# A depthwise convolution of 31 taps moved from the vector engine to the tensor engine, and a recurrence's inputs made ahead, in a two-layer hybrid backbone

## The chip, the cores and the metric

The kernel runs on one core of one Trainium2 chip. The metric is the device time of one execution in microseconds (us), as the median of several runs. The engines are TensorE (PE, with its weight loads as PEld), VectorE (DVE), ScalarE (ACT), GpSimd (POOL) and SyncE (SP), whose queue issues nearly all DMAs.

## The reference, cut to what matters

Each of two layers joins four groups of heads behind one input projection. Layer 0 has 1024 latent and 256 context tokens; layer 1 puts out the latent ones alone. The parts that the change touches are the recurrence (a), the convolution module (c), and around them the attention (b) and the Hyena inputs (d):

```python
p = h @ w_in[l]
y_a = rglru_mixer(p[..., :OFF_B], ...)       # short convolution, gates, scan in both directions
y_b = diff_attn_mixer(p[..., OFF_B:OFF_C], ...)
y_c = conformer_conv(p[..., OFF_C:OFF_D], *conf)
y_d = hyena_mixer(p[..., OFF_D:], ...)
...
def conformer_conv(pc, conv_w, conv_b, ln_g, ln_b, w_pw, b_pw):
    u = pc[..., :W_C] * jax.nn.sigmoid(pc[..., W_C:])        # W_C = 256 channels
    u = dwconv(u, conv_w, conv_b, (CONF_K // 2, CONF_K // 2))   # CONF_K = 31 taps, one filter a channel
    u = layer_norm(u, ln_g, ln_b)
    return jax.nn.silu(u) @ w_pw + b_pw
```

The context is convolved by itself, so zeros stand between it and the latent tokens. Behind these follow the output projection and a mixture of experts.

## The kernel before

Channels lie on the 128 partitions and tokens along the free axis. `phase1` (L2028) does the input projection, the recurrence and the attention of a layer. `win` (L1044) projects one block of 128 output channels: it loads 512 KB of weights (`wir`), splits them on ACT into a rounded high part `wih` and on POOL into the rest `wil`, and for each group of 512, 512 and 256 tokens issues 24 matmuls (8 slices of the inner dimension, three products of high and low parts) into one accumulator `mm`; a function given with it then evacuates the accumulator. In the projections there are five accumulators `mm`, and three named `rg` for the recurrence and what follows.

The order in the program is: block 0; the recurrence for channels 0 to 127 (`recur(0)`); blocks 12 and 10, then 13 and 11, whose evacuation `glu_evac` writes the gated linear unit into an SBUF tile `cu`; block 2 with `gate(0, h)`; block 1 and the recurrence for channels 128 to 255; queries, keys and values; `gate(1, h)`; and last `conv31` for both channel blocks.

`rglru` (L1377) goes through three pieces for each of two directions. In each it makes `rg_u` by a convolution of 4 taps (one instruction on POOL, three on DVE), multiplies it on PE with two gate matrices (L1407), and goes on over ACT, POOL and a scan on DVE. The tile `rg_u` has one buffer. `conv31` (L1444) runs 31 instructions on DVE over all tokens (1295 columns in layer 0, 1024 in layer 1), each adding one tap to `cacc`, and stores the result in `cd`, which `conformer` (L1464) reads later for the layer norm.

The attention (L1153) follows with its own accumulators and a single `mm`, which the Hyena rows 14 to 19 (`rest`, L2091) and in layer 0 a part of the next layer's modulation (`modulation`, L954, L979) use in turn. Behind it `hyena_in` (L1713) loads `hx`, convolves it on POOL and DVE into `hu` and transposes it on PE into an `rg` accumulator, and `conformer` and the Hyena transforms (`tabc`, `H`) follow.

The order of the instructions on each engine is made by a scheduler when the kernel is built: of the instructions that are ready by its own reckoning it takes the one that stands first in the program. So an instruction that stands late can run early where its engine has room. On the chip each engine then works strictly in its order.

## Time and profile before

| what | value |
|---|---|
| median of 3 runs | 3575.4 us (3574.82 to 3578.94) |
| profiled execution, time | 3583.19 us |
| profiled execution, span of its instructions | 3581.3 us |
| PE busy | 3073.7 us, 86% |
| DVE busy | 2274.8 us, 64% |
| ACT busy | 1564.7 us, 44% |
| POOL busy | 722.5 us, 20% |
| mean granted PE clock | 0.923 |

Busy time is the union of an engine's instructions. Ends of matmuls are modelled, so a busy PE isn't PE at its peak; the distance from one matmul's start to the next tells its pace. The granted clock is the share of PE's full clock in a stretch; its two levels are 1.2 and 2.4 GHz, 0.5 and 1.0. All times below are counted from the start of the span.

### The profile page before, as it was taken

What the parts mean: (1) busy time and instruction counts of PE and PEld (TensorE: products, weight loads), DVE (VectorE), ACT (ScalarE), POOL (GpSimd) and SP (SyncE); (2) the same over time, 40 slices, a digit from 0 to 9 for tenths busy, and PEclk for the clock granted to TensorE, in tenths of its full rate; (3) what the DMA queues carried; (4) which work ended last, traced back from release to release, by engine and by line L of the source; (5) the groups of instructions that cost most, each with busy time, mean ns of one, the idle gap of its engine ahead of it and who ended that gap; (6) DMA issues with size and microseconds to landing.
All of it is one profiled execution on the core that took longest, in us unless ns stands there. A gap on an engine that the chain in (4) does not pass through costs nothing. (4 is left out here: it accounts for less than half of the span.)

```text
span 3581.3 us, 43827 instructions
## 1 busy us (share of the span) xinstructions
PE 3073.7 (86%) x14952; PEld 2071.0 (58%) x14952; DVE 2274.8 (64%) x3297; ACT 1564.7 (44%) x2537; POOL 722.5 (20%) x579
## 2 busy tenths in 40 slices
PE   5798888997899699999997587799779799899993
PEld 1246665775678354676554465667657655465551
DVE  6674885787768433476543778588876653355626
ACT  4234334772334233455543444377323343344533
POOL 2212451003210111111110435300330111111102
PEclk8899899998999699999999798899899899999996
DMA  5752226215565888987878512311546489988796
GB/s 185 230 192 61 69 90 212 70 39 191 161 210 174 286 305 307 369 292 258 318 254 322 170 40 92 135 57 46 174 145 230 151 287 379 378 283 285 270 349 236
DMA packets 415375, 743.33 MB, mean 208 GB/s; under 512 B 46219, under 2 KB 181240, under 8 KB 415146
## 3 DMA queue, kind: packets, MB, share of 16 engines
q1 hardware_dynamic: 397546, 702.69, 56.6%
q0 software_dynamic: 17600, 37.79, 3.1%
q8 instruction: 119, 1.95, 0.2%
q14 instruction: 110, 0.90, 0.1%
HBM read 656.13 MB, written 105.30 MB: 213 GB/s over the span
## 5 line engine op out<-in xcount | busy, mean ns | idle before, releaser
L679 DVE TENSOR_TENSOR wl<-wr,wh 128x1024 fp32r<-128x1024 f32 (+1 forms) x440 | 516.2, 1203 | 395.8 <-ACT wh L678 382.8
L678 ACT ACTIVATE wh<-wr 128x1024 fp32r<-128x1024 f32 (+1 forms) x440 | 442.1, 1038 | 331.5 <-PE mm L730 192.6
L734 PE MATMUL mm<-wr,xl 128*64 128x512 f32 x1216 | 327.6, 607 | 3.4 <-DVE xl L690 1.6
L1065 PE MATMUL mm<-hh,wih 128*128 128x512 f32 (+1 forms) x752 | 290.6, 387 | 13.8 <-ACT stg L1129 8.3
L1065 PE MATMUL mm<-hh,wil 128*128 128x512 f32 (+1 forms) x752 | 289.4, 386 | 10.5 <-POOL wil L951 9.7
L730 PE MATMUL mm<-wh,xh 128*128 128x512 f32 x704 | 288.7, 411 | 6.8 <-ACT wh L678 6.2
L1065 PE MATMUL mm<-hl,wih 128*128 128x512 f32 (+1 forms) x752 | 289.9, 386 | 1.5 <-DVE hl L951 1.0
L730 PE MATMUL mm<-wl,xh 128*128 128x512 f32 x704 | 278.4, 395 | 3.9 <-DVE wl L679 3.8
L730 PE MATMUL mm<-wh,xl 128*128 128x512 f32 x704 | 277.4, 394 | 0.0
L790 POOL DMA_INDIRECT fd<-ot,ridx x82 | 94.3, 1150 | 843.0 <-ACT ot L786 261.0
L1451 DVE SCALAR_TENSOR_TENSOR cacc<-cu,cw,cacc 128x1295 f32<-128x1295 f32 (+1 forms) x120 | 194.5, 1621 | 1.9
L671 POOL DMA_INDIRECT gb<-h2d,ridx x82 | 98.3, 1199 | 466.9 <-PE tr L698 177.9
L730 PEld LDWEIGHTS mm<-wh,xh 128*128 128x128 f32 x704 | 133.0, 189 | 92.6 <-issue 45.1
L1199 DVE TENSOR_REDUCE m<-A 128x1 f32<-128x1024 f32 x128 | 156.2, 1220 | 44.6 <-PE A L1189 36.6
L951 POOL TENSOR_TENSOR wil<-wir,wih 128x1024 fp32r<-128x1024 f32 x34 | 92.5, 2722 | 431.0 <-ACT wih L948 375.3
L734 PEld LDWEIGHTS mm<-wr,xl 128*64 128x64 f32 x1216 | 95.2, 137 | 141.8 <-issue 124.4
L1065 PEld LDWEIGHTS mm<-hh,wih 128*128 128x128 f32 x752 | 147.0, 196 | 44.9 <-ACT stg L1129 11.9
L1065 PEld LDWEIGHTS mm<-hh,wil 128*128 128x128 f32 x752 | 147.5, 196 | 39.1 <-POOL wil L951 10.9
L1065 PEld LDWEIGHTS mm<-hl,wih 128*128 128x128 f32 x752 | 147.4, 196 | 30.8 <-issue 6.2
L780 PE MATMUL mm<-wr,hl 128*64 128x512 f32 x608 | 154.9, 604 | 0.0
L1244 ACT ACTIVATE wT<-TR 128x512 f32<-128x512 f32 (+1 forms) x200 | 104.9, 524 | 108.2 <-PE TR L1239 99.1
L730 PEld LDWEIGHTS mm<-wl,xh 128*128 128x128 f32 x704 | 133.6, 190 | 30.5 <-DVE wl L679 6.7
(491 smaller groups left out, 6527.4 us busy)
## 6 DMA issues: line engine op xcount, KB each, us to landing
wr<-in_moe_w_gate_dram SPq DMA_DIRECT2D x256, 512.0 KB
wr<-in_moe_w_up_dram SPq DMA_DIRECT2D x256, 512.0 KB
wr<-in_moe_w_down_dram SPq DMA_DIRECT2D x256, 512.0 KB
wada<-in_w_ada_dram SPq DMA_DIRECT2D x48, 512.0 KB
tabc<-in_k_t_c_dram SPq DMA_DIRECT2D x88, 256.0 KB
wir<-in_w_in_dram SPq DMA_DIRECT2D x40, 512.0 KB
wr<-in_w_ada_dram SPq DMA_DIRECT2D x32, 512.0 KB
ks<-qkd SPq DMA_DIRECT2D x16, 640.0 KB
```

What stands on the lines that cost most here:

```text
L671: self.K.nc.gpsimd.indirect_dma_start(out=g[s, :D // (1 + h)], out_offset=None, in_=self.h2d[h], in_offset=bass.IndirectOffsetOnAxis(ap=id ...
L678: nc.scalar.activation(hi, src, AF.Copy)
L679: nc.vector.tensor_tensor(lo, src, hi.bitcast(FT), op=OP.subtract)
L730: nc.tensor.matmul(ps[b][w], x(k), y[:, kk], start=(k == 0 and c == 0), stop=(k == 7 and c == 2))
L734: nc.tensor.matmul(ps[b][0][w * 64:(w + 1) * 64], self.XT[n0 + b](k), raw[w][:, kk], start=(k == 0), stop=(k == 7))
L780: nc.tensor.matmul(po[b][0][o * 64:(o + 1) * 64], HT[b][:, k], raw[:, o], start=(k == 0), stop=(k == 3))
L790: s = nc.gpsimd.indirect_dma_start(out=self.fd[h], out_offset=bass.IndirectOffsetOnAxis(ap=ridx[r], axis=0), in_=ot[r], in_offset=None, bo ...
L951: (eng or nc.vector).tensor_tensor(lo, src, hi.bitcast(FT), op=OP.subtract)
L1065: nc.tensor.matmul(p[:, :n], a[:, k], b[:, k, t0:t0 + n], start=(k == 0 and a is wh and b is hh), stop=(k == 7 and a is wl))
L1199: nc.vector.tensor_reduce(m[:, c, 1:2], A[c], axis=AX.X, op=OP.max, negate=True)
L1244: nc.scalar.activation(o, i_, AF.Copy)
L1451: nc.vector.scalar_tensor_tensor(a, u[:, j:j + N], cw(j), a, op0=OP.mult, op1=OP.add)
```

## The change

The 31 taps are applied on PE. The gated linear unit no longer stays in SBUF: `glu_evac` stores each group in a DRAM buffer `ud` with zeros before, between and behind the two token ranges. `conv31` goes in pieces of 256 tokens. It loads a piece four times, shifted by 0 to 3 tokens, so that the 128 rows of a matmul are 32 channels at four shifts; 8 such matmuls, 4 tokens apart, add up the taps for 32 channels, and four groups of 32 channels write to the four quarters of the accumulator's partitions. The weights (`taps`) are made on the chip: a transpose, and a product with a pattern of ones on POOL. Ten pieces in layer 0 and eight in layer 1, with two buffers `cu`, now stand behind the Hyena rows in the attention's part of the program. A DVE instruction adds the bias and evacuates.

The recurrence's 4-tap convolution is a function of its own, `rglru_conv`, with six buffers `rg_u`, and comes before the GLU blocks' projection; block 1 comes before the second GLU pair, and `gate(0)` moves behind the first queries, keys and values. `stg` has three buffers in place of two.

```diff
@@ setup
-        self.cd = self.dram.tile([2 * P, T0 + 15], FT, name="cd")
+        self.cd = self.dram.tile([2 * P, T0], FT, name="cd")
+        self.ud = self.dram.tile([2 * P, UW], FT, name="ud")
...
+        for o, n in ((0, 15), (15 + TL, 15), (30 + T0, 16)):
+            nc.sync.dma_start(self.ud[:, o:o + n].rearrange("(b p) t -> p b t", p=P), z[:, :, :n])
@@ glu_evac
-            nc.vector.scalar_tensor_tensor(u[:, o:o + n], th[0][:, :n], 1.0, p[:, :n], op0=OP.add, op1=OP.mult)
+            t = th[0][:, :n]
+            nc.vector.scalar_tensor_tensor(t, t, 1.0, p[:, :n], op0=OP.add, op1=OP.mult)
+            nc.sync.dma_start(self.ud[b * P:(b + 1) * P, o:o + n], t)
@@ rglru
+    PIECES = [[(TL, TL + 3, TC), (0, 0, 512), (512, 512, 512)], [(TL, TL + 3, TC), (512, 512, 512), (0, 0, 512)]]
+
+    def rglru_conv(self, l, w, b, xa):
+        nc, res = self.nc, []
+        for s in range(3):
+            for d in range(2):
+                t0, a, n = self.PIECES[d][s]
...
+                u = w.tile([P, 512], FT, name="rg_u", bufs=6)[:, :n]
+                nc.gpsimd.tensor_scalar(u, xa[:, o:o + n], cw(0), self.pc("a_conv_b", d * 2 + b), op0=OP.mult,
+                                        op1=OP.add)
+                for j in range(1, 4):
+                    nc.vector.scalar_tensor_tensor(u, xa[:, o + j:o + j + n], cw(j), u, op0=OP.mult, op1=OP.add)
+                res.append(u)
+        return res
...
-        h = [w.tile([P, T0], FT, name=f"h{d}") for d in range(2)]
+        h = [w.tile([P, T0], FT, name=f"h{d}", bufs=2 - d) for d in range(2)]
...
-                u, r, i, t = (w.tile([P, 512], FT, name="rg_" + x, bufs=1 + (x != "u"))[:, :n] for x in "urit")
-                nc.gpsimd.tensor_scalar(u, xa[:, o:o + n], cw(0), self.pc("a_conv_b", c), op0=OP.mult, op1=OP.add)
-                for j in range(1, 4):
-                    nc.vector.scalar_tensor_tensor(u, xa[:, o + j:o + j + n], cw(j), u, op0=OP.mult, op1=OP.add)
+                u = us[s * 2 + d]
+                r, i, t = (w.tile([P, 512], FT, name="rg_" + x, bufs=2)[:, :n] for x in "rit")
@@ conv31
-        a = w.tile([P, N], FT, name="cacc")
...
-        nc.vector.tensor_scalar(a, u[:, 0:N], cw(0), self.pc("c_conv_b", b), op0=OP.mult, op1=OP.add)
-        for j in range(1, 31):
-            nc.vector.scalar_tensor_tensor(a, u[:, j:j + N], cw(j), a, op0=OP.mult, op1=OP.add)
-        nc.sync.dma_start(self.cd[b * P:(b + 1) * P, :N], a)
+    def taps(self, l, b, w):
...
+        R = w.tile([32, 4, 32], FT, name="taps", bufs=1)
+        nc.gpsimd.memset(R, 0.0)
+        for j in range(8):
+            m = min(4, 31 - 4 * j)
+            nc.sync.dma_start(R[j * 4:(j + 1) * 4, :m], bass.AP(
+                tensor=cw.tensor, offset=cw.offset + 4 * j * 256 + b * P, ap=[[32, 4], [256, m], [1, 32]]))
+        p = self.psum_mm()
+        nc.tensor.transpose(p[:, :32], R.rearrange("r s c -> r (s c)"), self.ident[:32, :32])
+        t = w.tile([P, 32], FT, name="tapsT", bufs=1)
+        nc.scalar.activation(t, p[:, :32], AF.Copy, scale=0.5)
...
+        W = w.tile([P, 32, 32], FT, name="tapw", bufs=1)
+        nc.gpsimd.tensor_tensor(W, one[:, None, :].to_broadcast([P, 32, 32]), t[:, :, None].to_broadcast([P, 32, 32]),
+                                op=OP.mult)
+        return W
+
+    def conv31(self, w, x, b, W, t0, n):
+        nc = self.nc
+        u = self.ud[b * P:(b + 1) * P].rearrange("(g c) t -> c g t", g=4)
+        o = t0 + (15 if t0 >= TL else 0)
+        for s in range(4):
+            nc.sync.dma_start(x[s * 32:(s + 1) * 32], u[:, :, o + s:o + s + n + 28])
+        p = self.psum_mm()
+        for j in range(8):
+            for g in range(4):
+                nc.tensor.matmul(p[g * 32:(g + 1) * 32, :n], W[:, j * 4 + g], x[:, g, 4 * j:4 * j + n],
+                                 start=(j == 0), stop=(j == 7))
+        t = w.tile([P, 512], FT, name="stg", bufs=3)
+        nc.vector.tensor_scalar(t[:, :n], p[:, :n], self.pc("c_conv_b", b), None, op0=OP.add)
+        nc.sync.dma_start(self.cd[b * P:(b + 1) * P, t0:t0 + n], t[:, :n])
@@ phase1
-                    h = recur(0)
                     for b in range(2):
-                        u = wd.tile([P, N], FT, name="cu", bufs=2)
...
-                        self.win(l, w, [12 + b, 10 + b], hs, allg, self.glu_evac(wd, u))
-                        us.append(u)
-                    gate(0, h)
-                    h = recur(1)
+                        if b:
+                            xa, f = self.rglru_in(xap)
+                            self.win(l, w, [b], hs, GROUPS, [f])
+                            xs.append(xa)
+                        us = self.rglru_conv(l, rg, b, xs[b])
+                        self.win(l, w, [12 + b, 10 + b], hs, allg, self.glu_evac(wd, b))
+                        hs_.append(self.rglru(l, rg, b, us, prm, ctx_out))
...
-                        gate(1, h)
-                for b in range(2):
-                    self.conv31(l, wd, b, us[b], ctx_out)
+                            gate(i, hs_[i])
...
+                cv = self.pool(c2, "cv")
                 if l == 0:
                     t = [lambda: xap.tile([P, T0 + 9], FT, name="xa")] + \
-                        [lambda: wd.tile([P, N], FT, name="cu", bufs=2)] * 2
+                        [lambda: cv.tile([P, 1136], FT, name="cu", bufs=2)] * 2
...
                 rest(range(max(MAT, EARLY[l]), 6))
+                for b in range(2):
+                    W = self.taps(l, b, cv)
+                    for t0 in range(0, T0 if ctx_out else TL, 256):
+                        x = cv.tile([P, 1136], FT, name="cu", bufs=2).rearrange("p (g t) -> p g t", g=4)
+                        self.conv31(wd, x, b, W, t0, 256)
```

## Rows read from the trace of the kernel before

**Rows 1.** Busy us and instructions by engine in stretches; PE clock, DMA share, GB/s

```profile
core 0: us, PE busy (x) PEld busy (x) DVE busy (x) ACT busy (x) POOL busy (x), PEclk, DMA share, GB/s
277.00:562.00 285.00, 236.72 (x1178) 193.12 (x1176) 206.54 (x188) 113.31 (x154) 128.11 (x88) 0.92 0.26 86
...
578.00:835.00 257.00, 240.34 (x1725) 171.61 (x1725) 202.52 (x356) 177.51 (x438) 11.56 (x4) 0.98 0.25 79
835.00:905.00 70.00, 43.58 (x190) 36.15 (x191) 53.91 (x54) 13.77 (x27) 39.17 (x38) 0.76 0.75 248
2043.00:2300.00 257.00, 213.34 (x984) 168.39 (x984) 193.42 (x188) 114.29 (x154) 117.80 (x80) 0.90 0.22 73
2300.00:2320.00 20.00, 6.27 (x20) 4.28 (x19) 4.17 (x10) 4.85 (x11) 2.34 (x1) 0.63 0.77 263
2320.00:2340.00 20.00, 14.36 (x61) 9.69 (x62) 15.19 (x26) 9.17 (x23) 0.00 (x0) 0.51 0.07 21
...
2528.00:2600.00 72.00, 54.48 (x273) 45.05 (x274) 58.82 (x69) 19.77 (x36) 31.90 (x26) 0.86 0.68 216
```

**Rows 2.** Waits of PE in 277:562, then 2043:2316: total us, times, longest

```profile
PE rg L1407 <- DVE rg_u L1404: 35.5, 11, 6.3
...
PE rg L1407 <- DVE rg_u L1404: 38.7, 10, 7.0
```

**Rows 3.** Groups by shape on DVE in 277:562, then 2043:2300

```profile
L1451 DVE SCALAR_TENSOR_TENSOR cacc<-cu,cw,cacc 128x1295 f32<-128x1295 f32 x60 | 104.5, 1741 | 0.9
...
L1451 DVE SCALAR_TENSOR_TENSOR cacc<-cu,cw,cacc 128x1024 f32<-128x1024 f32 x60 | 90.0, 1500 | 1.0
```

**Rows 4.** Groups by shape on PE in 277:562, then 2043:2300

```profile
L1065 PE MATMUL mm<-hh,wil 128*128 128x512 f32 x200 | 82.2, 413 | 10.5 <-POOL wil L951 9.7 <-DVE wil L951 0.6
...
L1065 PE MATMUL mm<-hh,wih 128*128 128x256 f32 x96 | 28.7, 299 | 0.0
...
L1407 PE MATMUL rg<-rg_u,gw 128*128 128x512 f32 x32 | 21.9, 822 | 26.2 <-DVE rg_u L1404 26.2
...
L1065 PE MATMUL mm<-hh,wil 128*128 128x512 f32 x190 | 78.0, 411 | 0.0
...
L1065 PE MATMUL mm<-hh,wih 128*128 128x256 f32 x32 | 9.3, 292 | 0.2 <-DVE hh L950 0.2
```

**Rows 5.** Timeline of PE in 362:372: start, us, instruction

```profile
365.03 0.39 PE L1065 MATMUL mm<-hl,wih 128*128 128x512 f32 x1
...
365.94 0.39 PE L1065 MATMUL mm<-hh,wil 128*128 128x512 f32 x1
366.74 1.98 PE L1407 MATMUL rg<-rg_u,gw 128*128 128x512 f32 x4 [0.41 <-DVE rg_u L1404]
```

**Rows 6.** Busy time by stretch, the sum of 520:540 and 540:560

```profile
sum 40.00, PE 40.00 PEld 34.55 DVE 19.93 ACT 12.08 POOL 26.30; mean PE 20.00 PEld 17.27 DVE 9.96 ACT 6.04 POOL 13.15
```

**Rows 7.** Timeline of PE in 590:600, the modulation among the attention's matmuls

```profile
593.65 0.39 PE L979 MATMUL mm<-xa,sT 128*2 128x256 f32 x3
593.67 0.38 PE L979 MATMUL mm<-cu,sT 128*2 128x256 f32 x1
593.87 0.39 PE L979 MATMUL mm<-xa,sT 128*2 128x256 f32 x3
```

**Rows 8.** Timeline of PE in 642.5:644.3

```profile
642.84 1.09 PE L1257 MATMUL PO<-wT,vt 128*64 128x128 f32 x16
643.86 0.74 PE L1189 MATMUL A<-ks,qs 128*128 128x512 f32 x2
```

**Rows 9.** Line 1065 in 540:1000: min/median/max ns, first and last start

```profile
L1065 PE MATMUL mm<-hh,wil x172: 278/389/506, 539.9 to 834.7; 128*128 128x512 f32 x112, 128*128 128x256 f32 x60
```

**Rows 10.** Line 1476, the Conformer norm's first matmuls, layer 0 and layer 1

```profile
L1476 PE MATMUL rg<-cx,om x12: 379/592/1061, 902.4 to 938.2; 128*128 128x512 f32 x8, 128*128 128x256 f32 x4
...
L1476 PE MATMUL rg<-cx,om x8: 592/592/595, 2590.7 to 2608.0; 128*128 128x512 f32 x8
```

**Rows 11.** Line 1121, an evacuation on DVE, whole span

```profile
L1121 DVE SCALAR_TENSOR_TENSOR cu<-stg,mm x10: 410/676/689, 310.0 to 2120.6; 128x512 f32<-128x512 f32 x8, 128x256 f32<-128x256 f32 x2
```

**Rows 12.** The page's costliest groups

```profile
L951 POOL TENSOR_TENSOR wil<-wir,wih 128x1024 fp32r<-128x1024 f32 x34 | 92.5, 2722 | 431.0 <-ACT wih L948 375.3
```

More of the change, by code (lines that the diff above doesn't have):

```diff
@@ L855 @@
 C8 = math.sqrt(0.5)
+UW = T0 + 46
 GROUPS = [(0, 512, 0), (512, 512, 0), (1024, 256, 1)]
@@ L908, in setup @@
         self.yd = self.dram.tile([8, P, T0], FT, name="yd")
-        self.cd = self.dram.tile([2 * P, T0 + 15], FT, name="cd")
+        self.cd = self.dram.tile([2 * P, T0], FT, name="cd")
+        self.ud = self.dram.tile([2 * P, UW], FT, name="ud")
+        z = c.tile([P, 2, 16], FT, name="zeros")
+        nc.vector.memset(z, 0.0)
+        for o, n in ((0, 15), (15 + TL, 15), (30 + T0, 16)):
+            nc.sync.dma_start(self.ud[:, o:o + n].rearrange("(b p) t -> p b t", p=P), z[:, :, :n])
     def params(self, l, psum, R):
@@ L1109, in win_v, with glu_evac @@
             nc.scalar.activation(vt[:, b:b + 2].rearrange("p b c -> p (b c)"), p, AF.Copy)
-    def glu_evac(self, w, u):
+    def glu_evac(self, w, b):
         nc, th = self.nc, []
         def f(p, t0, n, v):
-            th[:] = [w.tile([P, 512], FT, name="stg", bufs=2)]
+            th[:] = [w.tile([P, 512], FT, name="stg", bufs=3)]
             nc.scalar.activation(th[0][:, :n], p[:, :n], AF.Tanh, scale=0.5)
@@ L1127, in f @@
         def f(p, t0, n, v):
-            q = w.tile([P, 512], FT, name="stg", bufs=2)
+            q = w.tile([P, 512], FT, name="stg", bufs=3)
             nc.scalar.activation(q[:, :n], p[:, :n], AF.Copy)
@@ L1416, in rglru @@
             for d in range(2):
-                t0, _, n = pair[d]
+                t0, _, n = self.PIECES[d][s]
                 a, i, t = st[d]
@@ L1436, in f @@
         def f(p, t0, n, v):
-            g = w.tile([P, 512], FT, name="stg", bufs=2)[:, :n]
+            g = w.tile([P, 512], FT, name="stg", bufs=3)[:, :n]
             nc.scalar.activation(g, p[:, :n], AF.Gelu_apprx_tanh)
@@ L1441, in rglru_out @@
         return f
[L1444 removed]
+    def taps(self, l, b, w):
         nc = self.nc
[L1446 to L1452 removed]
+        cw = self.I["c_conv_w"][l]
+        R = w.tile([32, 4, 32], FT, name="taps", bufs=1)
[8 more added lines that the diff above has]
+        nc.scalar.activation(t, p[:, :32], AF.Copy, scale=0.5)
+        one = w.tile([P, 32], FT, name="tap1", bufs=1)
+        nc.vector.tensor_reduce(one, self.ident.rearrange("p (s c) -> p c s", s=4), axis=AX.X, op=OP.add)
+        W = w.tile([P, 32, 32], FT, name="tapw", bufs=1)
[16 more added lines that the diff above has]
+        nc.sync.dma_start(self.cd[b * P:(b + 1) * P, t0:t0 + n], t[:, :n])
     def spread(self, p, r, t):
@@ L2046, in phase1 @@
                 wd = self.pool(c, "wd")
-                self.cw = self.keep.tile([P, 62], FT, name="cw")
-                a = self.col["c_conv_w"]
-                nc.vector.tensor_scalar(self.cw, self.pp[:, a:a + 62], 0.5, None, op0=OP.mult)
-                N = TL + 30 + (15 + TC if ctx_out else 0)
-                us = []
                 self.pr = self.pool(c2, "r_ps", 3, space=PSUM)
```

30 lines of the change are left out of this document (9 added, 21 removed).

## The prediction

> **What bounds the kernel now.** I read busy time by stretch first [rows 1], then who PE waited for [rows 2], then the groups by shape [rows 3, 4]. The whole span is a chain of stages that follow one another, so a stage that ends earlier moves everything behind it. The change touches three neighbouring stretches in each layer: the projections (277 to 562 us in layer 0, 2043 to 2300 in layer 1), the attention (578 to 835; to 2528), and the stretch behind it in which the Hyena inputs are made (835 to 905; 2528 to 2600).
>
> In the projections no engine looks full: PE 236.7 of 285 us, DVE 206.5 [rows 1]. But PE's clock there is 0.92 and 0.90, which says that PE keeps stopping, and the waits name the reason: PE stands before the recurrence's gate matmuls until DVE has made `rg_u`, 35.5 us in layer 0 and 38.7 in layer 1 [rows 2]. DVE is late because the 31-tap convolution runs through it all this time: 60 instructions for 104.5 us in layer 0, 60 for 90.0 in layer 1 [rows 3]. The tile `rg_u` has one buffer, so the next piece's convolution starts only when the last piece is through, and each of its few DVE instructions stands between 1.5 to 1.7 us ones of the long convolution. Where the convolution has ended, PE is full: 40.00 of 40 us [rows 6].
>
> How long would PE need alone? Back to back, from 365.03 to 365.94 lie four starts of a 512-column projection matmul, 0.227 us each [rows 5]; I price 256 columns at half of it, 0.114, an estimate. Four gate instructions take 1.98 us [rows 5], 0.5 each, half of that at 256 columns. Layer 0 by count [rows 4]: 3 x 200 x 0.227 = 136, 3 x 96 x 0.114 = 33, the values block's 240 (5 x 48 in the code) x 0.114 = 27, the gates' 32 x 0.5 + 16 x 0.25 = 20; together 216 of the 285 us. Layer 1: 568 x 0.227 = 129, (96 + 240) x 0.114 = 38, gates 20; 187 of 257. So 69 and 70 us are the price of waits and of the half clock that follows them.
>
> In the attention PE is busy 240 of 257 us at clock 0.98 [rows 1]; there is little room. In the stretch behind it PE is busy 43.6 of 70 us, and DVE, with 53.9, is the busiest.
>
> **The change, part by part.**
>
> *The DVE convolution goes.* That frees 104.5 + 90.0 us of DVE in the projections (and four first taps). DVE keeps about 100 us of work in each, well under PE's. The gain is not the DVE time but what PE lost: I let PE run at its own pace plus the weight waits that have another cause, 9.7 us behind POOL's `wil` [rows 4] and some 1.3 of smaller ones, 11 in all; I charge layer 1 the same though it shows less. Layer 0: 285 - 216 - 11 = 58. Layer 1: 257 - 187 - 11 = 59. Sum **-117 us**.
>
> *`rg_u` in six buffers, made ahead of the next projection block.* Same instructions, moved: 6 POOL and 18 DVE instructions for each block. They now come before the GLU block's projection, about 28 us of PE work that needs none of them, so a gate matmul finds its input made. What could be late next: the GLU evacuations queue on DVE behind those 18. By the long convolution's rate, 1.74 us for 1295 columns [rows 3], 512 columns are 0.7 us, so 12 us for all; PE has five accumulators to fill meanwhile, 5 x 24 x 0.227 = 27 us of work. I cost it at nothing; without that cover it is those 12 us in each of the four blocks.
>
> *The convolution on PE.* Each piece of 256 columns takes 32 matmuls, and a full fp32 matmul shows as two instructions here (24 gate calls in a layer, 48 instructions, 32 of them in [rows 4]). Ten pieces in layer 0 and eight in layer 1 make 640 + 512 = 1152 instructions. No row has 32-column weights. The nearest is the modulation (L979): fp32, 256 columns, four column groups in turn, as here. There four start within 0.02 us (593.65 and 593.67) and the next four 0.22 later (593.87) [rows 7]. So 288 groups of four x 0.215 = **62 us** of PE. Unpacked it would be 1152 x 0.213 = 245 us, the upper end; I take the packed price, by that row.
>
> The Trainium skill gives less for packing ("TensorE: Matmul & The Clock Gate", Part 3, measured speedup): three column tiles ran 2.38 times as fast, 79% of the ideal. By it the estimate would be 62 / 0.79 = 78 us instead of 62, and the result 16 us later if none of that is hidden. The trace shows no such loss at four tiles.
>
> *Where it lands.* In the program it stands behind the last Hyena projection row, and it shares the stage's single accumulator `mm` with those rows, which in layer 0 start their last matmul at 834.7 [rows 9]. So most of it falls behind the attention. PE is free there for 70 - 43.6 = 26 us and 72 - 54.5 = 18 us, and in layer 1 also at the start of the attention, 2300 to 2340, where PE is busy 20.6 of 40 us (19 free) [rows 1]. That is 63 us for 62. Its reader, the Conformer norm, starts at 902.4 and 2590.7 [rows 10], 67 and 63 us behind the end of the attention, and one layer needs 34 or 28 us of PE. A fit as exact as that doesn't come about: with one accumulator each piece waits for its evacuation, and engines keep their queue order. I take a third as exposed, **+20 us** (ends: 0 and 62).
>
> *Evacuation and stores.* 18 DVE instructions of 128x256 from PSUM, by the nearest row 0.41 us each (L1121's shortest) [rows 11]: 7 us, in the stretch where DVE is busiest; I charge all, **+7**. Queued behind each on DVE are the Hyena input taps, and PE's transposes wait for those.
>
> *Loads.* `conv31` reads four shifted copies: 4 x 32 x 4 x 284 x 4 bytes = 0.58 MB a piece, 10.5 MB in all, and 72 more issues on SP. At the 248 and 216 GB/s of the stretches behind the attention [rows 1] that is 45 us of transfers where DMA is already busy 0.75 and 0.68. Two `cu` buffers let one load run under the other piece's matmuls, so the bounds are 0 and 45; the free quarter to a third of 142 us, about 41, holds nearly all, and I take **+5**. SP is in order: a load that waits for its buffer holds the `tabc`, `H` and `hx` loads behind it. The 11 small stores of `ud`, the taps' tiny loads, two transposes and one POOL product of 128x1024 a layer and block lie beside other work; without cover one such product is 2.7 us, as POOL's `wil` of the same shape [rows 12], four times.
>
> *Gate 0 moved* behind the first query, key and value blocks: same work; `h0` gets a second buffer, so nothing waits.
>
> Sum: -117 + 20 + 7 + 5 = **-85 us**.
>
> **The rivals.**
>
> *B, the convolution is packed but nothing hides it:* the PE order puts the Hyena input's transposes behind it and the stretch grows by all of it. -117 + 62 + 7 + 10 = -38. For it: `hx` and `rg` buffers and DVE are already tight there. Against: 63 us of free PE.
>
> *C, slower: it is dealt out in small runs among the attention's matmuls.* A switch of array shape costs time: sixteen 64-column instructions from 642.84 keep a pace of 0.10 a pair, the last starts at about 643.66, and the next full-width one at 643.86, 0.20 later [rows 8]. So a switch costs about 0.1 us more, twice for each run. In runs of four: 288 x 0.2 = 58 us on top of 62, in a stage without room: -117 + 62 + 58 + 12 = +15. It decides from about 210 runs on, that is, runs under six instructions. For it: the attention is where the program puts it, and the modulation does run there in pieces of 2 to 4 [rows 7]. Against: the accumulator is taken by the projection rows till the attention ends.
> The Trainium skill has this as a rule ("TensorEngine Tiling (Array Packing)", Key Properties): changing the tiling mode drains the engine. The trace agrees with its 0.1 us; that speaks against C's place, not its price.
>
> *D, the projections don't become PE's:* the recurrence's own chain over ACT, POOL and DVE, or weight preparation on POOL (128 of 285 us busy), takes over and half the gain stays away: -58 + 32 = -26. Against: rows 6, with the same weights and PE full.
>
> *E, all hidden, and the free PE at 2320 to 2340, where the granted clock is 0.51 [rows 1], is filled, so the attention starts at the full level:* -117 + 7, and up to 5 more; about -115.
>
> **How the numbers follow.** The profiled execution took 3583.2 us (span 3581.3); the median of the runs is 3575.4, 7.8 less. So the likeliest is 3575.4 - 85 = 3490 us, its own range 3460 to 3525. B 3537, C 3590, D 3549, E 3460. Chances: mine 0.56, B 0.17, C 0.08, D 0.10, E 0.09. The range of 3450 to 3562 leaves out C and some of the tails. 0.2% is 7 us, about what a measurement of this kernel can tell from no change: faster 0.89 (all but C and the poorest ends of B and D), same 0.03, slower 0.08.
>
> **What would show it.** Right: in the projections the wait of the gate matmuls for `rg_u` is below 5 us a layer, PE's clock 1.0, and the stretch from the first projection to the first score matmul is some 58 us shorter in each layer; `conv31`'s matmuls start four by four at 0.215; the Conformer norm starts no later behind the attention than 67 and 63 us. Wrong: a longer attention with runs of few convolution instructions in it (C), a stretch of Hyena inputs that grows by 30 us (B), or gate matmuls that still wait, now for ACT or POOL (D).

## The result and the profile after

The changed kernel takes 3615.6 us (median of four runs, 3601.65 to 3620.42) against 3575.3 for the kernel before beside it: ratio 1.0107, 95% interval 1.0091 to 1.0122. It is some 40 us slower, where 85 us less were forecast. The profiled execution took 3620.42 us, its span 3618.3, which is 37.0 more than before.

Busy time by stretch, after (the columns are those of [rows 1]):

```profile
core 0: us, PE busy (x) PEld busy (x) DVE busy (x) ACT busy (x) POOL busy (x), PEclk, DMA share, GB/s
278.00:533.00 255.00, 221.13 (x1160) 183.52 (x1159) 97.62 (x126) 97.42 (x143) 111.25 (x82) 0.94 0.29 94
550.00:803.00 253.00, 236.96 (x1723) 170.05 (x1721) 200.73 (x357) 176.81 (x438) 11.83 (x10) 0.99 0.27 84
803.00:925.00 122.00, 81.48 (x833) 57.12 (x834) 56.64 (x65) 13.61 (x29) 39.39 (x36) 0.89 0.63 193
2065.00:2295.00 230.00, 196.13 (x922) 159.47 (x921) 102.54 (x126) 95.37 (x139) 106.32 (x80) 0.90 0.23 76
2295.00:2320.00 25.00, 16.81 (x68) 12.77 (x66) 4.79 (x7) 4.11 (x6) 2.39 (x1) 0.86 0.66 227
2320.00:2340.00 20.00, 10.79 (x30) 6.53 (x30) 15.22 (x23) 11.11 (x26) 2.34 (x1) 0.50 0.40 105
2532.00:2640.00 108.00, 79.77 (x751) 56.69 (x750) 62.71 (x76) 18.97 (x37) 36.69 (x33) 0.91 0.60 180
```

Against [rows 1] DVE in the projections has fallen from 206.5 to 97.6 us and from 193.4 to 102.5, as the prediction said. But these windows have shortened by 30 and 27 us only, and PE's granted clock in them is 0.94 and 0.90 (0.92 and 0.90 before), not 1.0. From the last projection row's last matmul to the Conformer norm's first it is now 120 us (68 before), and 104 in layer 1 (64 before). No engine is full there: of the 122 us from 803 PE is busy 81, DVE 57, and DMA 0.63.

Waits of PE in the projections, 278 to 533 and 2065 to 2310 (us in total, times, longest):

```profile
PE mm L1072 <- POOL wil L958: 14.8, 3, 11.4
PE mm L1072 <- ACT wih L955: 14.4, 2, 11.0
PE rg L1429 <- ACT rg_i L1430: 3.2, 1, 3.2
...
PE mm L1072 <- POOL wil L958: 12.4, 2, 9.3
PE mm L1114 <- ACT wvh L955: 6.3, 2, 4.3
PE mm L1114 <- POOL wvl L958: 5.7, 2, 5.0
PE rg L1429 <- ACT rg_r L1430: 4.1, 2, 2.1
PE mm L1072 <- ACT wih L955: 3.0, 1, 3.0
```

The waits for `rg_u` of [rows 2] are gone. In their place PE waits for the projections' weights, which POOL and ACT split (`wih`, `wil`, and `wvh`, `wvl` of the values block): 29 us in layer 0, 27 in layer 1. The 11.4 us stall is read from POOL's timeline:

```profile
356.02 5.41 POOL L1398 TENSOR_SCALAR rg_u<-xa,pp 128x256 f32<-128x256 f32 x4
361.40 3.03 POOL L1452 TENSOR_TENSOR h<-h,h 128x1280 f32<-128x1280 f32 x1
364.42 3.12 POOL L1398 TENSOR_SCALAR rg_u<-xa,pp 128x512 f32<-128x512 f32 x2
367.51 2.76 POOL L958 TENSOR_TENSOR wil<-wir,wih 128x1024 fp32r<-128x1024 f32 x1
```

The six `rg_u` instructions made ahead stand in POOL's queue before `wil`, and PE gets its weights only behind them. Behind the attention, PE's timeline (start, duration; in brackets the idle time before and what ended it):

```profile
805.66 3.66 PE L1501 MATMUL mm<-cu,tapw 128*32 128x256 f32 x64 [2.27 <-POOL tapw L1486]
809.93 3.66 PE L1501 MATMUL mm<-cu,tapw 128*32 128x256 f32 x64 [0.61 <-DVE stg L1504]
817.48 5.35 PE L1501 MATMUL mm<-cu,tapw 128*32 128x256 f32 x64 [3.89 <-DMA cu<-ud]
...
855.36 3.66 PE L1501 MATMUL mm<-cu,tapw 128*32 128x256 f32 x64 [0.60 <-DVE stg L1504]
858.95 0.66 PE L1790 MATMUL rg<-ident,hu 128*128 128x128 f32 x4
865.80 3.59 PE L1790 MATMUL rg<-ident,hu 128*128 128x128 f32 x16 [6.19 <-DVE stg L1504]
```

A piece of 64 instructions takes 3.66 us, so the packed rate came out. But the ten pieces run as one block, 3.66 us of work in some 5.5 us each, and the first transposes of the Hyena inputs (L1790) stand behind the tenth. What PE waited for between the pieces, 803 to 870 and 2532 to 2590 (busy us, mean ns, then idle us and what ended it):

```profile
L1501 PE MATMUL mm<-cu,tapw 128*32 128x256 f32 x640 | 38.3, 393 | 16.5 <-DMA cu<-ud 9.4 <-POOL tapw L1486 4.6 <-DVE stg L1504 2.5
...
L1501 PE MATMUL mm<-cu,tapw 128*32 128x256 f32 x512 | 33.5, 412 | 13.6 <-DMA cu<-ud 10.5 <-DVE stg L1504 2.7 <-POOL tapw L1486 0.4
```

That is 30 us in both layers, 20 of them for the pieces' loads. SP's timeline shows the other half:

```profile
850.50 1.39 SPq L1497 DMA_DIRECT2D cu<-ud  x3
855.34 0.34 SPq L1505 DMA_DIRECT2D cd<-stg  x1
855.72 0.43 SPq L1773 DMA_DIRECT2D hx<-pd  x1
856.19 0.44 SPq L1775 DMA_DIRECT2D hx<-pd  x1
```

The loads `hx` of the second Hyena block issue at 855.7, behind all loads `cu` (which wait for a buffer) and nine of the ten stores `cd` (which wait for an evacuation).

### The profile page after: what moved, and what is told of

Read it like the earlier page. It is cut to its first block, busy times and chain, and to the rows that moved or that the text cites. A ratio compares the mean times of both kernels' runs of the same rounds, so it can differ in the third digit from the quotient of the medians.

```text
span 3618.3 us, 46274 instructions
## 1 busy us (share of the span) xinstructions
PE 3119.8 (86%) x16108; PEld 2099.0 (58%) x16108; DVE 2088.0 (58%) x3194; ACT 1534.6 (42%) x2521; POOL 700.0 (19%) x577
## 5 line engine op out<-in xcount | busy, mean ns | idle before, releaser
L1072 PE MATMUL mm<-hh,wil 128*128 128x512 f32 (+1 forms) x752 | 287.7, 383 | 27.8 <-POOL wil L958 27.2
L1208 DVE TENSOR_REDUCE m<-A 128x1 f32<-128x1024 f32 x128 | 156.2, 1221 | 41.8 <-PE A L1198 32.5
L730 PEld LDWEIGHTS mm<-wh,xl 128*128 128x128 f32 x704 | 133.4, 190 | 28.9
```

Source lines behind the costliest of these rows:

```text
L730: nc.tensor.matmul(ps[b][w], x(k), y[:, kk], start=(k == 0 and c == 0), stop=(k == 7 and c == 2))
L1072: nc.tensor.matmul(p[:, :n], a[:, k], b[:, k, t0:t0 + n], start=(k == 0 and a is wh and b is hh), stop=(k == 7 and a is wl))
L1208: nc.vector.tensor_reduce(m[:, c, 1:2], A[c], axis=AX.X, op=OP.max, negate=True)
```

## The experiments

All kernels follow the same chain of stages, so each is told by the lengths of three of them, in layer 0 and layer 1, read from the starts of PE's instructions: from the first projection matmul to the first score; from there to the last projection row's last matmul; from there to the first matmul of the output projection. The lengths come from one profiled execution of each kernel. Where two kernels share a stage they agree within 2 us in the projections of layer 0 and behind the attention, within 5 in the attention, and only within 8 in the projections of layer 1 (285.9 to 293.9); what lies around the stages is 2133 to 2148 us. "Ratio" is to the kernel before on the same chip (3574.5 to 3579.3), with its interval. Differences in the text are of medians; by the ratios they come out up to 5 us other.

| kernel | median us | ratio | projections | attention | behind it |
|---|---|---|---|---|---|
| before | 3575.3 | 1 | 300.8, 309.1 | 256.6, 213.5 | 185.8, 167.7 |
| changed | 3615.6 | 1.0091 to 1.0122 | 271.1, 291.9 | 252.9, 214.5 | 239.3, 205.6 |
| e1 no convolution | 3520.2 | 0.9827 to 0.9880 | 271.3, 289.1 | 254.7, 213.4 | 187.5, 166.1 |
| e3 first tap on DVE | 3597.5 | 1.0030 to 1.0074 | 261.6, 280.4 | 255.9, 214.5 | 238.6, 204.7 |
| e2 before, two `rg_u` | 3560.3 | 0.9944 to 0.9979 | 293.5, 302.7 | 256.2, 213.4 | 186.8, 168.1 |
| e10 before, inputs ahead | 3560.3 | 0.9950 to 0.9980 | 289.0, 297.1 | 264.6, 214.8 | 183.6, 167.6 |
| e11 e10, first tap on DVE | 3549.2 | 0.9921 to 0.9955 | 281.9, 288.4 | 261.2, 216.7 | 185.5, 166.8 |
| e4 pieces behind inputs | 3630.5 | 1.0109 to 1.0187 | 270.2, 290.3 | 253.8, 212.8 | 253.1, 216.6 |
| e6 pieces in projections | 3607.9 | 1.0078 to 1.0118 | 315.6, 319.8 | 264.9, 213.1 | 183.9, 165.9 |
| e7 pieces in attention | 3652.6 | 1.0201 to 1.0248 | 271.5, 287.9 | 329.8, 264.4 | 185.1, 166.1 |
| e5 `cu` on ACT's queue | 3603.2 | 1.0054 to 1.0094 | 271.5, 293.9 | 252.0, 215.0 | 229.9, 203.9 |
| e9 one load | 3586.4 | 1.0024 to 1.0055 | 271.4, 286.3 | 252.4, 213.1 | 217.3, 200.0 |
| e12 full width | 3598.3 | 1.0048 to 1.0081 | 271.0, 287.7 | 254.5, 214.4 | 234.2, 200.0 |
| e13 dealt between | 3624.0 | 1.0105 to 1.0146 | 271.5, 289.3 | 254.1, 213.4 | 249.7, 206.6 |
| e14 e13, one load | 3583.4 | 0.9992 to 1.0022 | 270.1, 291.8 | 253.5, 214.4 | 221.0, 191.6 |
| e16 e13, `hx` on POOL's queue | 3620.5 | 1.0084 to 1.0126 | 270.1, 288.8 | 256.3, 213.2 | 244.0, 211.3 |
| e17 `hx` on POOL's queue | 3607.3 | 1.0058 to 1.0092 | 270.8, 289.2 | 253.2, 214.5 | 227.2, 207.2 |
| e18 e13, `cu`, `cd` on ACT's queue | 3585.0 | 1.0009 to 1.0031 | 269.6, 285.9 | 253.4, 212.9 | 225.1, 192.1 |
| e15 e13, first tap on DVE | 3606.1 | 1.0060 to 1.0106 | 261.0, 279.3 | 255.3, 213.1 | 250.7, 208.1 |
| e19 e18, first tap on DVE | 3567.8 | 0.9962 to 0.9986 | 261.2, 279.1 | 254.6, 213.2 | 225.5, 193.7 |

### What the convolution costs, and what the projections gain

e1: the pieces give way to a copy in DRAM.

```diff
-                for b in range(2):
-                    W = self.taps(l, b, cv)
...
+                nc.sync.dma_start(self.cd[:, :TL], self.ud[:, 15:15 + TL])
+                if ctx_out:
+                    nc.sync.dma_start(self.cd[:, TL:T0], self.ud[:, 30 + TL:30 + T0])
```

> The changed kernel without the convolution: the pieces and their weights are left out, and cd gets the unfiltered linear unit by one copy for each token range, so the output is not the reference's. Theory (the convolution stands alone between the Hyena rows and the Hyena inputs, 803 to 866 and 2536 to 2586 us in the changed kernel, and hides nothing): 85 to 95 us faster than the changed kernel, 3520 to 3530, and the Hyena inputs end some 65 us behind the last row again, as before the change. Rival (the stretch is long for another reason, a changed order or the stores of ud, and the pieces are covered): less than 30 us faster, above 3585.

It took 95 us off the changed kernel, nearly all of it behind the attention, where the stage returned to its lengths of before (187.5 and 166.1). So the convolution on PE, with its loads, evacuations and stores, costs 51.8 + 39.5 = 91 us there; the rest of the change is worth 56.

e2 gives the kernel before a second buffer, e3 the changed kernel another engine for the first tap:

```diff
-                u, r, i, t = (w.tile([P, 512], FT, name="rg_" + x, bufs=1 + (x != "u"))[:, :n] for x in "urit")
+                u, r, i, t = (w.tile([P, 512], FT, name="rg_" + x, bufs=2)[:, :n] for x in "urit")
...
-                nc.gpsimd.tensor_scalar(u, xa[:, o:o + n], cw(0), self.pc("a_conv_b", d * 2 + b), op0=OP.mult,
+                nc.vector.tensor_scalar(u, xa[:, o:o + n], cw(0), self.pc("a_conv_b", d * 2 + b), op0=OP.mult,
```

> The kernel before with a second buffer for rg_u and nothing else. Theory (the single buffer is what makes the gate matmuls late): the gate matmuls' wait for rg_u falls from 74 to under 40 us, and the time by 15 to 30, to 3545 to 3560. Rival (the long convolution's instructions in DVE's queue are what makes them late, whatever the buffers): waits above 60 us, time within 7 us of 3575.

> The changed kernel with the first tap of the recurrence's convolution on DVE in place of POOL, one word changed. Theory (the six POOL instructions made ahead stand in POOL's queue before the weight remainder wil, and PE waits 11.4 and 9.3 us for it at one block in each layer): those two waits fall below 3 us, 15 to 25 us faster than the changed kernel, 3590 to 3600. Rival (the weights come late by ACT's queue or by the two weight buffers): the waits move to ACT, less than 7 us.

e2 took 15 us off the kernel before, 13.7 in the projections. But PE's waits for `rg_u` fell from 74 to 56 us only (23.4 in 272 to 560 and 33.0 in 2030 to 2305), not under 40: a second buffer is a part of the cause. e3 took 18 off the changed one: 9.5 and 11.5 in the projections, and PE's wait for `wil` there fell from 14.8 to 5.3 us and from 12.4 to 3.0. So the step of making `rg_u` ahead did cost something, through POOL's queue.

e10 is half of the change: `rglru_conv`, six buffers and the order of blocks and gates are those of the changed kernel, the convolution stays on DVE (some pools moved to make room). e11 adds e3's step.

> Half of the change alone: the kernel before, its 31-tap convolution left on the vector engine, with six buffers for the recurrence's inputs made ahead of the next projection blocks, and the order of blocks and gates of the changed kernel (some pools lie elsewhere to make room). A second buffer alone gave 15 us. Theory O (the loss of the change sits in the tensor engine's convolution and its loads behind the attention, the gain of some 30 and 17 us at the end of the projections comes from the inputs ahead and the freed vector engine): 3515 to 3550, and the wait of the gates for their inputs is gone; the vector engine, with 206 of some 255 us, doesn't yet bound. Rival (the freed vector engine makes the whole gain): 3555 to 3580, since the 18 instructions made ahead then stand among the long convolution and delay the evacuations of the gated linear unit.

> As the kernel with the inputs ahead and the vector engine's convolution, with the first tap of the inputs made on the vector engine, so that the weight preparation on GpSimd has nothing in front of it. Theory O: 10 to 18 us less than that kernel, as the same step took 18 us off the changed one. Rival (there the vector engine is the bound and the preparation is hidden): no difference, or up to 6 us more, for 12 instructions of some 0.4 us a layer on it.

e10 came out at 3560, at the rival's lower end: the projections are 11.8 and 12.0 us shorter than before, and the attention of layer 0 is 8 longer, which wasn't followed up. PE's waits in its first projections (278 to 560) and its busy time there:

```profile
PE rg L1419 <- ACT rg_i L1420: 10.6, 3, 5.3
PE mm L1107 <- ACT wvh L948: 8.3, 2, 4.6
PE mm L1107 <- POOL wvl L951: 6.2, 2, 5.6
...
278.00:552.00 274.00, 237.08 (x1175) 195.53 (x1174) 210.04 (x187) 99.23 (x142) 127.47 (x87) 0.91 0.26 86
```

No gate matmul waits for `rg_u` any more, with DVE as busy as before (210 us), and yet only 12 of the 35.5 us of [rows 2] are gained: other waits have come up. Against e10 the changed kernel, with DVE free, is another 17.9 and 5.2 us shorter. So the DVE convolution's removal is worth some 23 us in the projections once the inputs are ahead (the 5.2 of layer 1 lie within the 8 by which that stage varies). e11 took 11 more, to 3549: 0.6% under the kernel before, and the fastest kernel here with a convolution.

### The place of the pieces

e4 moves them behind the Hyena inputs in the program, e6 to the end of the projections (with the first tap on DVE and fewer buffers for the modulation), e7 into the attention, ahead of its projection rows.

```diff
@@ e4, behind the last hyena_in and ahead of the conformer (e6: in phase1, ahead of the attention; e7: behind it)
+                    cv = self.pool(c2, "cv")
+                    for b in range(2):
+                        W = self.taps(l, b, cv)
+                        for t0 in range(0, T0 if ctx_out else TL, 256):
+                            x = cv.tile([P, 1136], FT, name="cu", bufs=2).rearrange("p (g t) -> p g t", g=4)
+                            self.conv31(cv, x, b, W, t0, 256)
```

> The changed kernel with the convolution moved behind the six Hyena inputs in the program, with the five accumulators of that part. Theory (in the changed kernel the loads of the pieces and PE's order hold the Hyena inputs back, while PE and DVE have room): the inputs end some 65 us behind the last row as before the change, the pieces run beside them, 50 to 75 us faster than the changed kernel, 3540 to 3565. Rival (the pieces' own DMAs or PE time are the price, wherever they stand): less than 20 us faster.

> The changed kernel with the convolution at the end of the projections, with their five accumulators and ahead of the attention in the program, the state tile h0 in another pool so that the pieces' tiles come free early, the modulation of layer 1 with two tiles in place of three, and the first tap of the recurrence on DVE. Theory (a late place in the projections fills PE's waits there, and no stretch behind it is held up): the pieces start before the last projection, cost at most their packed 62 us and less by what they fill, the stretch behind the attention is 65 us again, 3530 to 3565. Rival (the pieces cost their 95 us in any place where PE's order is full): 3590 or more.

> The changed kernel with the convolution ahead of the modulation and the Hyena rows in the attention's part of the program. Theory (the prediction's case C: the pieces are dealt out among the attention's matmuls in small runs, and each run costs two changes of array shape): the attention and rows take 60 us longer in layer 0 and 45 in layer 1, the stretch behind is 65 us again, 3600 to 3650. Rival (the attention leaves PE enough room, and only the place behind it was bad): the attention longer by under 20 us a layer, 3550 to 3570.

In e4 the inputs were early again, and the pieces ran alone behind them, with the Hyena transforms behind the pieces. PE's timeline of e4:

```profile
870.35 8.34 PE L1501 MATMUL mm<-cu,tapw 128*32 128x256 f32 x128
880.94 7.12 PE L1501 MATMUL mm<-cu,tapw 128*32 128x256 f32 x128 [2.26 <-DMA cu<-ud]
...
898.15 9.77 PE L1501 MATMUL mm<-cu,tapw 128*32 128x256 f32 x128 [4.33 <-DMA cu<-ud]
```

In e6 the block moved to the projections and took 54 and 39 us there (against e3), as much as behind the attention; the attention of layer 0, whose modulation has a tile less there, is 9 longer too. In e7 the stretch behind the attention has its old length, and the attention is 76.9 and 49.9 us longer. There the pieces are dealt out in short runs:

```profile
600.39 0.63 PE L1501 MATMUL mm<-cu,tapw 128*32 128x256 f32 x4
600.95 0.55 PE L1248 MATMUL TR<-ident,E 128*128 128x128 f32 x3
...
605.43 0.63 PE L1501 MATMUL mm<-cu,tapw 128*32 128x256 f32 x6
605.99 0.55 PE L1248 MATMUL TR<-ident,E 128*128 128x128 f32 x3
...
607.15 0.62 PE L1501 MATMUL mm<-cu,tapw 128*32 128x256 f32 x2
```

Four instructions hold PE for 0.56 us until the next matmul starts, and six as long; at the block's rate they would take 0.23 and 0.34. Rival C's place and its sign are right for e7, and its sum, 62 + 58 us and 12 for evacuations and loads, is near the 127. But that is luck: in e7's trace the 1152 instructions stand in 112 runs of 2 to 32, not 288 of four, and they hold PE for 99.8 us in all, 34 above the block's 66 and not 58. The other 27 us of the 127 weren't followed up.

### Loads, and the order at the build

e5 issues the loads `cu` from ACT's queue, e9 loads only a channel block's first piece (all pieces work on that tile), e12 has one full matmul for each four narrow ones.

```diff
@@ e5
-            nc.sync.dma_start(x[s * 32:(s + 1) * 32], u[:, :, o + s:o + s + n + 28])
+            nc.scalar.dma_start(x[s * 32:(s + 1) * 32], u[:, :, o + s:o + s + n + 28])
@@ e9
-        for s in range(4):
+        for s in range(0 if t0 else 4):
@@ e12
-            for g in range(4):
-                nc.tensor.matmul(p[g * 32:(g + 1) * 32, :n], W[:, j * 4 + g], x[:, g, 4 * j:4 * j + n],
-                                 start=(j == 0), stop=(j == 7))
+            nc.tensor.matmul(p[:, :n], W[:, j * 4:j * 4 + 4].rearrange("p g c -> p (g c)"),
+                             x[:, j % 4, 4 * j:4 * j + n], start=(j == 0), stop=(j == 7))
```

> The changed kernel with the pieces' loads issued from ACT's queue, one word changed. Theory S (SP's queue holds the Hyena input's loads behind the pieces' loads, which wait for a buffer): hx loads issue right behind the last row, the inputs run beside the pieces and end 15 to 30 us earlier in each layer, 3555 to 3585. Theory O (the pieces stand first in the order of PE and DVE as well, and the inputs would wait there): less than 15 us, above 3600.

> The changed kernel with only the first piece of each channel block loaded; the other pieces use the same tile again, so most of the convolution's input is left out. PE and DVE work are the same. Theory S (loads in SP's queue are the price): the stretch behind the last row falls back to nearly 65 us, 60 to 85 us faster than the changed kernel, 3530 to 3555. Theory O (order on PE and DVE): only the waits for loads go, about 14 us in layer 0 and 12 in layer 1, 20 to 30 faster, 3585 to 3595.

> The changed kernel with one matmul of 128 columns in the place of each four of 32 columns: it leaves out three of the four groups of channels (and adds the wrong taps), and its loads, accumulators, evacuations, stores and program order stay. By the gate matmuls (two instructions, 0.5 us each at 512 columns) a piece's 8 matmuls take 8 x 2 x 0.25 = 4 us on the chip, against the 3.66 us that the 32 packed ones take in the changed kernel, so the work on the tensor engine is the same; only the order at the build can differ, since a reckoning that doesn't know packing counts 32 matmuls one after another for the packed piece and 8 for this one. Theory O (the order is made by that reckoning, and the pieces run as a block ahead of the Hyena inputs since they seem too long to be dealt in): the Hyena inputs come forward, the Conformer norm starts about 20 us earlier in each layer, and the time is 40 to 60 us under the changed kernel, 3555 to 3575. Rival (the place in the program alone puts the pieces first, whatever they seem to cost): less than 15 us under the changed kernel, 3600 or more.

e5 took 12 us off the changed kernel and e9 29 (22.0 and 5.6 behind the attention), both as theory O had it. e12 took 17, and its pieces still ran as one block ahead of the transposes. PE's timeline of e12:

```profile
858.68 3.72 PE L1500 MATMUL mm<-cu,tapw 128*128 128x256 f32 x16 [0.58 <-DVE stg L1503]
864.07 3.69 PE L1500 MATMUL mm<-cu,tapw 128*128 128x256 f32 x16 [1.66 <-DMA cu<-ud]
867.60 1.62 PE L1789 MATMUL rg<-ident,hu 128*128 128x128 f32 x10
```

So the idea that the scheduler's reckoning of 32 narrow matmuls holds the inputs back fell, at 17 us instead of 40 to 60, though its rival had less than 15. Of the 17, 11 lie behind the attention (5.1 and 5.6); what they are wasn't followed up.

### Dealt out between the Hyena inputs

e13 puts one piece behind each of the first two Hyena input blocks and two behind each other one until none is left, with four buffers `cu`, two `tapw` and five accumulators; e14 is e13 with e9's single load. `some(n)` issues the next n pieces.

```diff
+                    W = [self.taps(l, b, cv) for b in range(2)]
+                    todo = [(t0, b) for t0 in range(0, T0 if ctx_out else TL, 256) for b in range(2)]
...
                     for b in range(2):
                         self.hyena_in(l, hc, b, ut, ctx_out)
+                        some(1)
...
                     for b in range(2, 6):
                         self.hyena_in(l, hc, b, ut, ctx_out)
+                        some(2)
```

> The changed kernel with the pieces dealt out: the taps are made at the start of the stage behind the attention, then one piece stands behind each of the first two Hyena input blocks and two behind each of the other four, token groups first, with four load buffers and the stage's five accumulators. Theory P (place: wherever the pieces stood as a block, the Hyena inputs behind them in the queues of TensorE, SyncE and the vector engine had to wait, and where they stood behind the inputs they ran alone): between the inputs the 62 us of TensorE and most of the loads are covered, the Conformer norm starts 75 to 90 us behind the last row in layer 0 (120 in the changed kernel, 67 before), and the time is 3535 to 3565. Rival Q (bandwidth: the loads take transfer time from the Hyena inputs wherever they stand): one load only took 29 us off the changed kernel, so dealing out gives back less than 15 us and the time is 3600 or more.

> The kernel with the pieces dealt out, with only the first piece of each channel block loaded; the other pieces convolve that first piece's tokens again, so their convolution of the right tokens is left out. Theory P: the loads are then mostly hidden already, so 0 to 10 us less than the kernel with the pieces dealt out. Rival Q: 25 us less or more.

e13 gave nothing (3624), against the theory of place; e14 gave 40, as its rival of transfers said. But the transfers weren't short of room. Busy time of e13 behind 860, and SP's timeline there:

```profile
860.00:928.00 68.00, 43.81 (x560) 26.27 (x560) 18.54 (x19) 5.88 (x12) 12.72 (x14) 0.78 0.43 116
...
872.38 0.34 SPq L1506 DMA_DIRECT2D cd<-stg  x1
872.76 0.43 SPq L1774 DMA_DIRECT2D hx<-pd  x1
...
881.08 0.34 SPq L1506 DMA_DIRECT2D cd<-stg  x1
881.46 2.35 SPq L1498 DMA_DIRECT2D cu<-ud  x5
889.84 0.34 SPq L1506 DMA_DIRECT2D cd<-stg  x1
890.27 0.38 SPq L1774 DMA_DIRECT2D hx<-pd  x1
```

DMA is busy 0.43 there. Each pair of `hx` loads follows a store `cd` at once: SP stood at the store until a piece was evacuated, and every load behind it stood too. A block takes 17 us, of which PE works 10. Three kernels test that:

```diff
@@ e16 (in e13) and e17 (in the changed kernel), both loads hx
-        nc.sync.dma_start(x[:, 1:1 + TL], self.pd[b * P:(b + 1) * P, 0:TL])
+        nc.gpsimd.dma_start(x[:, 1:1 + TL], self.pd[b * P:(b + 1) * P, 0:TL])
@@ e18 (in e13), the load as in e5, and
-        nc.sync.dma_start(self.cd[b * P:(b + 1) * P, t0:t0 + n], t[:, :n])
+        nc.scalar.dma_start(self.cd[b * P:(b + 1) * P, t0:t0 + n], t[:, :n])
```

> The kernel with the pieces dealt out between the Hyena inputs, with the loads hx issued from GpSimd's queue in the place of SyncE's. In the dealt-out kernel each hx load stood on SyncE behind a store cd that waits for a piece (at 872, 890 and 907 us the next load followed the store), so that a block took 17 us, in which DMA was busy 0.33 to 0.55. Theory S (SyncE's order: a load of the next block can't start before the last pieces are through): without that a block takes some 10 us by TensorE's work (2.4 for the transposes, 7.7 for two pieces), three blocks in layer 0 give back 20 us and layer 1 some 15, so 3580 to 3595. Rival Q (transfers: the bytes of the loads cost their time): within 10 us of the dealt-out kernel, 3614 or more.

> The changed kernel, with only the loads hx issued from GpSimd's queue in the place of SyncE's. In the changed kernel the loads of the second block stood on SyncE behind all of the convolution's loads and stores until 855.7 us. Theory S with TensorE's order beside it: the first two blocks are loaded and convolved early, but their transposes still stand behind the tenth piece on TensorE, so 10 to 20 us less than the changed kernel, 3595 to 3605, as the loads cu from ScalarE's queue gave 12. Theory S alone: 3560 to 3585. Rival Q: no difference from the changed kernel.

> The kernel with the pieces dealt out, with the convolution's loads cu and stores cd issued from ScalarE's queue in the place of SyncE's, so that SyncE's queue holds the Hyena loads alone. Theory S: as the kernel with the loads hx from GpSimd's queue, 3580 to 3595, or some 10 us more where ScalarE's evacuations ut then wait behind a store. Rival Q: within 10 us of the dealt-out kernel, 3614 or more.

e18 gave 39 us with the same bytes, so it is the queue and not the bandwidth. e16 gave nothing clear (4 us), against theory S; SP's waits say why. The first row is e13, the second e16, both 860 to 928:

```profile
SPq L1506 <- DVE stg L1505: 45.7, 7, 10.6
```

```profile
SPq L1506 <- DVE stg L1505: 33.8, 5, 13.8
```

Taking `hx` out of the queue leaves the stores in it, and behind them the Hyena tables and the next pieces' loads. PE's wait for `hu` fell from 32.5 us in e13 to 9.3 in e16 (805 to 927), but 10.2 us of waits for `cu` and 8.2 for the tables `tabc` came up instead. In e18 SP has no wait for `stg`. Busy time of e18 by stretch:

```profile
799.00:860.00 61.00, 36.80 (x273) 27.92 (x271) 44.52 (x49) 6.48 (x14) 31.52 (x36) 0.84 0.93 258
860.00:892.00 32.00, 31.33 (x434) 19.32 (x435) 11.62 (x16) 7.24 (x15) 9.06 (x7) 0.94 0.70 204
```

DMA is busy 0.93 ahead of 860 (0.70 in e13 from 804), and then PE is full, 31.3 of 32 us. e17 gave 8 us, all in layer 0, where 10 to 20 were expected: in the block order PE's queue holds the transposes anyway.

The last two add the first tap on DVE:

> The kernel with the pieces dealt out, with the first tap of the recurrence's inputs made on the vector engine, so that the weight preparation on GpSimd has nothing in front of it. That step took 18 us off the changed kernel, in the projections, a stage that the dealing doesn't touch: 12 to 20 us less here too, 3520 to 3550 by theory P, 3585 by rival Q.

> The kernel with the pieces dealt out and their loads and stores on ScalarE's queue, with the first tap of the recurrence's inputs made on the vector engine: the two causes found so far taken away together. Each acts in its own stage, so they add up: the step on the first tap took 18 us off the changed kernel and 18 off the dealt-out one, so 3565 to 3573, the first kernel with the convolution on TensorE under the kernel before (3575 to 3579). Rival (the attention or TensorE in the stretch behind it gives the gain back): 3580 or more. Neither expects it under the kernel with the vector engine's convolution, the inputs ahead and their first tap on the vector engine (3549).

e15 took 18 off e13, as expected where the stage is another. e19, with both causes removed, took 3567.8: 0.3% under the kernel before, but 13 to 19 us over e11 (by the ratios and by the medians), which leaves the convolution on DVE.

## Why the prediction was wrong

The spans differ by +37.0 us. By the table that is -29.7 - 17.2 in the projections, -2.7 in the attention, +53.5 + 37.9 behind it, and -4.7 around them. Forecast were -117 and +32 for the first and the third. Two steps failed, by some 70 and 60 us.

**"I let PE run at its own pace plus the weight waits that have another cause, ... 11 in all"** (the -117). The waits of [rows 2] were read as a price, 285 to 227 us. The gate waits did vanish, as said. But e10 shows that making the inputs ahead alone removes them for 12 us a layer, and that freeing DVE beyond it is worth some 23 in both. PE didn't come to its own pace: the weight waits didn't stay at 11 a layer, they came to 29 and 27, the gate matmuls waited another 4.1 and 5.6 us for ACT, and that pace was priced at the full clock, where 0.94 and 0.90 were granted (by 6% of 255 and 10% of 230 us at most 15 and 23 us, an estimate).

One part is shown: **"I cost it at nothing"** named the GLU evacuations on DVE as what could be late, and not `wil`, which stands behind the six instructions on POOL (e3: 21 us in the projections). This was rival D's weight preparation on POOL; its counterargument, [rows 6], held no recurrence beside it: the last gate matmul before starts at 516.0, [rows 6] at 520. The other part, some 50 of the 70 us, is argued only: in e3 the wait for ACT's `wih` is still 15.0 us in layer 0, and ACT's `wih` stands among the recurrence's activations in the timeline. Taking that wait away, and those of layer 1, wasn't tried.

**"I take a third as exposed"** (+20) and **"That is 63 us for 62."** Next to nothing was hidden, in any place tried (e4, e6, e7, e13, e18). Alone the 18 pieces are 18 x 3.66 = 66 us of PE. With the Hyena inputs free of SP's waits (e18) the convolution still costs 225.1 - 187.5 + 192.1 - 166.1 = 64 us. That what PE had free there lay in waits of the Hyena chain, and couldn't be filled without delaying that chain, is argued from this and not shown.

In the changed kernel another 28 come on top (91 - 64). Within the block PE stands idle between the pieces for 30 us, 20 of them for `cu`: that was the loads' term, **"+5"**, whose bound of 45 us was taken from bandwidth. How the 28 divide between these waits and the late loads `hx` no run separates. The prediction wrote that a load that waits for its buffer holds those behind it on SP, and gave it no price. e18 prices it at 39 us in the dealt-out order, with loads and stores off SP; e14, without most loads, gives 40. By these runs the two locks, PE's order and SP's, sit one behind the other: PE's order alone (e13) gives nothing, SP's alone 12 (e5) or 8 (e17), both together 31 (e18 against the changed kernel). The Trainium skill ("DMA: Bandwidth & Descriptors", Issuing engines are not separate DMA queues) says that starting DMAs from several engines saves only the time to initiate them, usually small; here moving loads and stores to a second engine gave 39 us (e13 to e18), since the store that SP waited at held up the loads behind it.

**Rival B** had the mechanism, with 79 us for what grew by 91, and **D** the projections' loss: it left -58 of the -117, and -47 came. They were priced as exclusive cases; together they give +21 (D's -58 and B's 62 + 7 + 10), against +37 measured. That is why the range missed. **C** didn't come about here; in e7 its place costs what it said, but not by its count. **E** is excluded: the stretch behind the attention grew, and the granted clock at 2320 to 2340 is 0.50 still.

**Right** were the packed rate, the count and price of the evacuations (0.48 us each for 0.41), the vanishing of the `rg_u` waits, and the place behind the last projection row. The rate of the pack is 4 to 1: 64 narrow instructions take 3.66 us and 16 full ones 3.69 (e12). That is above what the Trainium skill has for three column tiles ("TensorE: Matmul & The Clock Gate", Part 3, measured speedup: 2.38 times); here the measurement decides, as [rows 7] had it.

**Open** are why the pieces can't be covered by the rest of the Hyena work even in e18, whether e18's remaining 64 us would shrink with other orders of the transforms, and e12's 17 us. e18's trace says where to look in layer 0: its Conformer norm starts 91.8 us behind the last row against 69.1 in e1, so eight pieces (29 us of PE) cost 23 up to there, and the other 15 of the 37.6 us arise behind it, where only two pieces (7 us) run.

## What to carry to other kernels

A wait that the profile names is the last of several, so its length doesn't give the gain (12 us for 35.5 in e10): before a wait is booked as gained, ask which queue the next late thing stands in, and put the moved instructions into every in-order queue that they join. Idle time of an engine behind a serial chain was no room for new work here; price a moved block at its serial time unless rows show who runs beside it. Loads and stores of a new stage that wait for buffers or results should not share an in-order queue with loads that a later stage wants early. Where two causes can happen together, their sum belongs in the range.

## What was unexpected of the hardware

Four 32-column matmuls side by side cost no more than one of 128 columns on the same columns of data: 3.66 us against 3.69 for a piece. Dealt out in short runs among the attention's matmuls they lose it. In e7 a run of 2, 4, 6 or 8 instructions holds PE equally long until the next matmul starts, for 0.55 to 0.57 us (the medians of 23, 22, 12 and 9 runs); 16 hold it for 1.00 and 32 for 1.86 us. All runs together hold it for 99.8 us, for 66 us of work.
